# Attention heads taken two at a time: paired score matmuls, V as the stationary operand, outputs that arrive transposed

## The chip, the cores and the metric

The kernel runs on one core of one Trainium2 chip. The metric is device time in microseconds. A core has a matmul engine (PE, its weight loads listed apart as PEld), a vector engine (DVE), an activation engine (ACT), a general engine (POOL) and DMA queues (SP issues them); each executes its own instructions strictly in the order in which they were written to its queue, and waits on semaphores for the others.

## The reference

Two layers of an encoder on 256 tokens of width 1024. A layer is a half-step SwiGLU, a mixer, cross-attention to 256 memory tokens, a second half-step SwiGLU and a norm. Only the mixer and the cross-attention are touched here:

```
h = RMSNorm(x); z = h @ W_in                      # split among three groups of heads
A (mla): 8 heads, q and k of 96 columns, v of 64  # full softmax
B (swa): 4 heads of 64, 2 key heads, distance bias, one sink logit per head in the softmax sum
C (na):  4 heads of 64, neighbourhood bias per head
o = concat(RMSNorm(o_A, 512), RMSNorm(o_B, 256), RMSNorm(o_C, 256)) * g
x = x + o @ W_out
x = x + softmax(norm(q) norm(k)^T) v @ w_o        # 4 heads over 256 memory tokens
```

Every RMSNorm over a group divides a token's row by the root of its mean square over that group's columns.

## The kernel before

Everything stands in SBUF with 128 partitions; a 256 x 256 score matrix of a head is held as `[128, 2, 256]` (two blocks t of 128 queries, 256 keys). Weights come from memory as fp32 (`raw`) and are split on the chip into a high part (`whi`, ACT, line 140) and a low part (`wlo`, DVE, line 141); a product with weights is three matmuls (lines 167 to 169, and 528 to 530). The program is written in Python against a scheduler: each statement gives an instruction to an engine, and the scheduler fixes one order for each engine ahead of time. PSUM accumulators come from a pool of 8 (`acc`), 256-column working tiles from a pool of 8 (`b2`).

A layer l has a mixer (names `mx0...`, `mx1...`) and a memory attention (`me0...`, `me1...`); `kv0`, `kv1` is the memory's key and value projection, whose matmuls are interleaved with the mixer as hooks. In the mixer, `attend` goes through 16 heads in the order sw00, sw01, sw10, sw11 (swa), na00 to na11, ml00 to ml31 (mla). Head i's scores are issued at step i, the four 128 x 128 transposes of its probabilities at step i + d1 = i + 3, its products with V at step i + d2 = i + 5.

One head: two score matmuls into PSUM (`sc`, 64 rows of the array for swa, na and memory heads, 96 for mla). For swa and na the bias is added and the row maximum taken by one custom instruction for each t (line 447, into the separate tile `sb` and `mx`); for mla and memory by one reduction (line 441); `ng` is the negated maximum. ACT forms `p = exp(s - max)` in two calls (line 454) and, for swa, `es`, the sink's term (line 457). PE transposes p into `pt`; DVE copies it to `pT` in two copies (lines 467, 468). `values` then multiplies with pT as the stationary operand and V, 65 columns wide with a column of ones, as the moving one; so the softmax sum comes out as column 64. `finish`, once for two heads, takes the reciprocal `rc` and scales the output into `o` `[token, head column]` (line 418): nothing on DVE between a head's maximum and the next head's maximum depends on ACT.

`group_norm` squares o on ACT (line 844), forms the factor `om` on DVE (848) and `or` on POOL (line 173, a power), and scales o on DVE (852). `group_transposed` turns o over on PE (`ot`, line 864) and splits it into `oh` and `ol` (lines 176, 177). The table `AT` gives the steps at which these stand: norms at 9 and 12, transposes at 11 and 14; the norm of group A after the last head and its transposes inside the output projection. `project` multiplies with W_out (`mo`). The memory attention is the same with four heads a00, a01, a10, a11, outputs turned at line 930, split at 931 and 932, and `wo` as projection.

Of the kernel before, what the change touches and what calls it, by code (L numbers as in the profile page):

```python
# [9 lines left out]
F32 = mybir.dt.float32  # L10
# [8 lines left out]
P = 128  # L19
# [11 lines left out]
    d1=3, d2=5, look=3, norm1=9, turn1=11, norm2=12, turn2=14, turn0=20,  # L31
    keys=2, ksteps=3, knorm=3, kturn=13, v0=0, v1=13, e1=2, e2=4, wturn0=7, wturn1=6,
# [36 lines left out]
def encoder_kernel(ctx: ExitStack, tc: tile.TileContext, gxT, memT, wst, bparams, consts, nab, out):  # L69
# [36 lines left out]
    cmean = cp.tile([P, 3], F32, name="cmean")  # L106
    nc.vector.memset(cmean[:, 0:1], 1.0 / D)
    nc.vector.memset(cmean[:, 1:2], 1.0 / 256)
    nc.vector.memset(cmean[:, 2:3], 1.0 / 128)
    nhalf = cp.tile([P, 16], F32, name="nhalf")  # L110
# [284 lines left out]
    class Pair:  # L395


        def __init__(self, nm, o, cols):
            self.nm, self.o, self.cols = nm, o, cols
            self.pv, self.es = None, [None, None]  # L400

        def out(self, c):
            if self.pv is None:
                self.pv = acc(self.nm + "pv")[:, 0:260].rearrange("p (t c d) -> p t c d", t=2, c=2)
            return self.pv[:, :, c, :]

        def finish(self):
            pv = self.pv
            rc = small(4, self.nm + "rc").rearrange("p (t c) -> p t c", t=2)
            if self.es[0] is not None:  # L410
                dn = small(4, self.nm + "dn").rearrange("p (t c) -> p t c", t=2)
                for c in range(2):
                    nc.vector.tensor_tensor(dn[:, :, c], pv[:, :, c, 64], self.es[c], ALU.add)
                nc.vector.reciprocal(rc, dn)
            else:
                nc.vector.reciprocal(rc, pv[:, :, :, 64])
            for c in range(2):
                nc.vector.tensor_tensor(
                    self.o[:, :, self.cols[c], :], pv[:, :, c, 0:64], bc(rc[:, :, c], 64), ALU.mult
                )  # L420

    class Head:
        def __init__(self, pair, c, qT, kT, V, vh, prep=None, bias=None, sink=None):
            self.pair, self.c, self.qT, self.kT, self.V, self.vh = pair, c, qT, kT, V, vh
            self.prep = prep or (lambda: None)
            self.bias, self.sink = bias, sink
            self.nm = f"{pair.nm}{c}"
# [6 lines left out]
        def scores(self):  # L434
            nm = self.nm
            sc = acc(nm + "sc").rearrange("p (t k) -> p t k", t=2)
            for t in range(2):
                nc.tensor.matmul(sc[:, t, :], self.qT[:, t * P : (t + 1) * P], self.kT, start=True, stop=True)
            ng = small(2, nm + "ng")
            if self.bias is None:  # L440
                nc.vector.tensor_reduce(ng, sc, AX.X, ALU.max, negate=True)
                src = sc
            else:
                src = tp.tile([P, 2, T], F32, tag="b2", bufs=8, name=nm + "sb")
# [7 lines left out]
            self.p = tp.tile([P, 2, T], F32, tag="b2", bufs=8, name=nm + "p")  # L452
# [17 lines left out]
        def values(self):  # L470
            pv = self.pair.out(self.c)
            for t in range(2):
                for kt in range(2):
                    nc.tensor.matmul(
                        pv[:, t, :], self.pT[:, kt, t * P : (t + 1) * P], self.V[:, kt, self.vh, :],
                        start=kt == 0, stop=kt == 1,
                    )
            if self.c == 1:
                self.pair.finish()

    def attend(heads, hooks={}, d1=AT["d1"], d2=AT["d2"]):

        n = len(heads)
        heads[0].prep()
        for i in range(n + d2):
            if i + 1 < n:
                heads[i + 1].prep()
            if i < n:
                heads[i].scores()
                if i + 3 < n:  # L490
                    heads[i + 3].load()
            if 0 <= i - d1 < n:
                heads[i - d1].transposes()
            if 0 <= i - d2 < n:
                heads[i - d2].values()
# [48 lines left out]
    memV = cp.tile([P, 2, 4, 65], F32, name="memV")  # L544
    nc.gpsimd.memset(memV[:, :, :, 64:65], 1.0)
    memkT = cp.tile([P, 2, T], F32, name="memkT")

    class Memory:
# [62 lines left out]
        def values(self, n):  # L611
            if not self.at:
                self.ps = []
            self.steps("kvv", n, lambda t, ps: nc.scalar.activation(
                memV[:, t, :, 0:64], hd(ps[:, 0:256], 4), AF.Copy, scale=rmem[:, t : t + 1]
            ))

    def mixer(l, nx, mem):
# [32 lines left out]
        V = slot([P, 2, 14, 65], F32, nm + "V")  # L651
        nc.gpsimd.memset(V[:, :, :, 64:65], 1.0)
# [99 lines left out]
        for g in range(2):  # L752
            w = slice(512 * g, 512 * g + 512)
            for t in range(2):
# [8 lines left out]
                else:  # L763
                    nc.scalar.activation(V[:, t, 0:8, 0:64], hd(ps, 8), AF.Copy, scale=st)
# [69 lines left out]
        for h in heads[:3]:  # L834
            h.load()
# [295 lines left out]
```

## Time and profile before

| | us |
|---|---|
| median of 3 runs (lowest, highest) | 1047.52 (1047.47, 1062.58) |
| profiled execution | 1048.1 |
| its span, first to last instruction | 1046.3 |
| PE busy | 1024.0 (98%) |
| DVE busy | 718.0 (69%) |
| ACT busy | 556.7 (53%) |
| POOL busy | 114.2 (11%) |

The mean granted TensorE clock is 0.996 of full speed. In layer 0 the mixer's attention begins with its first score matmul at 236.29 us, the output projection runs from 282.79 to 307.03, the memory attention's projection begins at 331.10. In layer 1 the same points are at 752.91, 798.46, 822.70 and 846.65.

### The profile page before, as it was taken

Reading aid. Unit: us, or ns where it says so; the run is one execution under the profiler, and the core shown is the slowest. Engines: PE = TensorE matmul, PEld = TensorE weight load, DVE = VectorE, ACT = ScalarE, POOL = GpSimd, SP = SyncE. Lnnn points to the kernel's source line nnn. Section 1 sums busy time; section 2 is a strip of 40 time slices with the busy share of each in tenths; the row PEclk is TensorE's granted clock in tenths of the full one; section 3 lists DMA queues with packets and bytes.
Section 4 is the critical chain, followed back from the end, with each engine's and each line's share of the span. In section 5 each row is a group of like instructions: output and inputs, shape, how many; then the busy total and the mean of one; then the engine's idle time right before and its main releaser. Section 6 shows DMA issues by size and latency. Waiting matters only on the chain.

```text
span 1046.3 us, 20916 instructions
## 1 busy us (share of the span) xinstructions
PE 1024.0 (98%) x8480; PEld 1002.4 (96%) x8480; DVE 718.0 (69%) x1249; ACT 556.7 (53%) x928; POOL 114.2 (11%) x107
## 2 busy tenths in 40 slices
PE   8999999999999999999999999999999999999996
PEld 7999999998998999999999999999889999999996
DVE  7866667778786676666757666667886777766652
ACT  5755455566563565555545444546675546554541
POOL 4000000072031400000000000002600313000000
PEclk9999999999999999999999999999999999999998
DMA  8866666655042655555555555655531517666641
GB/s 277 276 208 192 198 199 206 186 173 182 22 136 67 234 189 199 188 199 192 192 184 187 188 186 184 206 186 167 181 131 32 172 38 241 204 189 196 194 130 41
DMA packets 54529, 181.79 MB, mean 174 GB/s; under 512 B 6048, under 2 KB 8992, under 8 KB 54432
## 3 DMA queue, kind: packets, MB, share of 16 engines
q1 hardware_dynamic: 54432, 180.45, 54.2%
q8 instruction: 66, 1.08, 0.4%
q14 instruction: 31, 0.25, 0.1%
HBM read 179.38 MB, written 1.05 MB: 172 GB/s over the span
## 4 chain that ended last, share of the span: by engine, by line
PE 72%; issue 17%; DVE 4%; POOL 2%; DMA 2%; ACT 2%; SPq 0%; POOLq 0%; DVEq 0%; ACTq 0%
PE f11i L169 4%; PE f11i L167 4%; PE f11i L168 4%; PE f01i L169 3%; PE f01i L167 3%; PE f01i L168 3%; PE f02i L168 3%; PE f02i L167 3%; PE f02i L169 3%; PE f11o L169 2%; PE f11o L167 2%; PE f11o L168 2%; PE f02o L169 2%; PE f01o L169 2%; PE f02o L168 2%
## 5 line engine op out<-in xcount | busy, mean ns | idle before, releaser
L141 DVE TENSOR_TENSOR wlo<-raw,whi 128x1024 fp32r<-128x1024 f32 (+4 forms) x337 | 407.5, 1214 | 208.9 <-ACT whi L140 207.7
L140 ACT CAST whi<-raw 128x1024 fp32r<-128x1024 f32 (+4 forms) x337 | 343.8, 1024 | 345.1 <-issue 86.0
L167 PE MATMUL f11i<-n10h,whi 128*128 128x256 f32 x320 | 90.1, 282 | 0.0
L168 PE MATMUL f11i<-n10l,whi 128*128 128x256 f32 x320 | 89.8, 281 | 0.0
L169 PE MATMUL f11i<-n10h,wlo 128*128 128x256 f32 x320 | 89.8, 281 | 0.0
L167 PE MATMUL f02i<-n20h,whi 128*128 128x256 f32 x320 | 88.5, 277 | 0.0
L167 PE MATMUL f01i<-n0h,whi 128*128 128x256 f32 x320 | 88.5, 277 | 0.0
L167 PE MATMUL f12i<-n21h,whi 128*128 128x256 f32 x320 | 88.5, 277 | 0.0
L169 PE MATMUL f01i<-n0h,wlo 128*128 128x256 f32 x320 | 88.4, 276 | 0.0
L168 PE MATMUL f02i<-n20l,whi 128*128 128x256 f32 x320 | 88.3, 276 | 0.0
L168 PE MATMUL f12i<-n21l,whi 128*128 128x256 f32 x320 | 88.3, 276 | 0.0
L169 PE MATMUL f02i<-n20h,wlo 128*128 128x256 f32 x320 | 88.3, 276 | 0.0
L168 PE MATMUL f01i<-n0l,whi 128*128 128x256 f32 x320 | 88.3, 276 | 0.0
L169 PE MATMUL f12i<-n21h,wlo 128*128 128x256 f32 x320 | 88.3, 276 | 0.0
L168 PEld LDWEIGHTS f11i<-n10l,whi 128*128 128x128 f32 x320 | 61.4, 192 | 0.0
L168 PEld LDWEIGHTS f12i<-n21l,whi 128*128 128x128 f32 x320 | 60.1, 188 | 0.0
L168 PEld LDWEIGHTS f02i<-n20l,whi 128*128 128x128 f32 x320 | 60.1, 188 | 0.0
L168 PEld LDWEIGHTS f01i<-n0l,whi 128*128 128x128 f32 x320 | 60.1, 188 | 0.0
L167 PEld LDWEIGHTS f01i<-n0h,whi 128*128 128x128 f32 x320 | 60.1, 188 | 0.0
L167 PEld LDWEIGHTS f11i<-n10h,whi 128*128 128x128 f32 x320 | 60.1, 188 | 0.0
L169 PEld LDWEIGHTS f01i<-n0h,wlo 128*128 128x128 f32 x320 | 60.1, 188 | 0.0
L167 PEld LDWEIGHTS f02i<-n20h,whi 128*128 128x128 f32 x320 | 60.1, 188 | 0.0
(1026 smaller groups left out, 2940.4 us busy)
## 6 DMA issues: line engine op xcount, KB each, us to landing
raw<-in_w SPq DMA_DIRECT2D x311, 512.0 KB, 4.2
raw<-in_w SPq DMA_DIRECT2D x12, 384.0 KB, 3.7
raw<-in_w SPq DMA_DIRECT2D x8, 416.0 KB, 3.3
kv0mt<-in_mem SPq DMA_DIRECT2D x8, 128.0 KB, 4.3
kv1mt<-in_mem SPq DMA_DIRECT2D x8, 128.0 KB, 3.7
gx<-in_gx SPq DMA_DIRECT2D x3, 256.0 KB, 7.2
out<-gx SPq DMA_DIRECT2D x3, 256.0 KB, 2.8
gx<-in_gx SPq DMA_DIRECT2D x1, 323.0 KB, 3.2
```

The costliest lines, as they stand in the source:

```text
L140: ins = nc.scalar.copy(hi[:, a:b], r[:, a:b])
L141: nc.vector.tensor_tensor(lo[:, a:b], r[:, a:b], hi[:, a:b].bitcast(F32), ALU.subtract)
L167: nc.tensor.matmul(ps, ah, bh, start=first, stop=False)
L168: nc.tensor.matmul(ps, ah, bl, start=False, stop=False)
L169: return nc.tensor.matmul(ps, al, bh, start=False, stop=last)
```

## The change

`Pair` now owns both heads of a pair. It issues the score matmuls of the two heads alternately (t = 0 of both, then t = 1 of both); for heads of 64 columns they lie in the two row halves of the array. `values` makes V (64 columns) stationary and pT (256 columns) moving, one head into PSUM partitions 0 to 63 and the other into 64 to 127; the result is `[feature, token]`, transposed from the outset. V and memV lose their column of ones. The softmax sum `dn` comes from the exponential's accumulator (`accum_out`); swa adds `es`; `rc` is taken for each head right after its exponentials, and p is multiplied by it in place, in two calls for each head, on POOL in the mixer and on DVE in the memory attention. The biased scores are written to p instead of `sb`. pT is copied in one instruction of 512 columns.

The outputs' own transposes (`ot`) are gone. The group norm now squares each pair's output on ACT (`osq`) beside a DVE copy to o, sums over features with matmuls of one column (`og`), forms `om` on DVE and `or` on POOL, spreads `or` over all partitions by two PE transposes (`ob`), and then multiplies on DVE and splits on ACT and DVE. Its hooks stand at steps 10 and 14, and inside the projection for group A. Rows of W_out and their gains are permuted on the host to the order in which the pairs put the heads.

```diff
+def mixed_order():
+    return np.concatenate([np.arange(512)] + [512 + 64 * h + np.arange(64) for h in (0, 2, 1, 3)] + [np.arange(768, 1024)])
...
-    d1=3, d2=5, look=3, norm1=9, turn1=11, norm2=12, turn2=14, turn0=20,
-    keys=2, ksteps=3, knorm=3, kturn=13, v0=0, v1=13, e1=2, e2=4, wturn0=7, wturn1=6,
+    d1=3, d2=5, look=3, norm1=10, norm2=14, norm0=4,
+    keys=2, ksteps=3, knorm=3, kturn=13, v0=0, v1=13, e1=2, e2=4,
...
+        def scores(self):
+            for h in self.heads:
+                h.sc = acc(h.nm + "sc").rearrange("p (t k) -> p t k", t=2)
+            for t in range(2):
+                for h in self.heads:
+                    nc.tensor.matmul(h.sc[:, t, :], h.qT[:, t * P : (t + 1) * P], h.kT, start=True, stop=True)
+            for h in self.heads:
+                h.weights()
+        def values(self):
+            pv = acc(self.nm + "pv")[:, 0:T]
+            for kt in range(2):
+                for c, h in enumerate(self.heads):
+                    nc.tensor.matmul(
+                        pv[64 * c : 64 * c + 64, :], h.V[:, kt, h.vh, :], h.pT[:, kt, :],
+                        start=kt == 0, stop=kt == 1,
+                    )
+            self.done(pv)
...
+            dn = small(2, nm + "dn")
             for t in range(2):
-                nc.scalar.activation(self.p[:, t, :], src[:, t, :], AF.Exp, bias=ng[:, t : t + 1])
+                nc.scalar.activation(
+                    self.p[:, t, :], src[:, t, :], AF.Exp, bias=ng[:, t : t + 1], accum_out=dn[:, t : t + 1]
+                )
             if self.sink is not None:
                 es = small(2, nm + "es")
                 nc.scalar.activation(es, ng, AF.Exp, bias=self.sink)
-                self.pair.es[self.c] = es
+                nc.vector.tensor_tensor(dn, dn, es, ALU.add)
+            rc = small(2, nm + "rc")
+            nc.vector.reciprocal(rc, dn)
+            for t in range(2):
+                self.eng.tensor_scalar(self.p[:, t, :], self.p[:, t, :], rc[:, t : t + 1], None, ALU.mult)
...
-            nc.vector.tensor_copy(self.pT[:, 0, :], ps[:, 0:T])
-            nc.vector.tensor_copy(self.pT[:, 1, :], ps[:, T : 2 * T])
+            nc.vector.tensor_copy(self.pT, ps.rearrange("p (k t) -> p k t", k=2))
...
+        def done(i):
+            def f(pv):
+                nc.vector.tensor_copy(o[:, i, :], pv)
+                osq[i] = b1(f"{nm}osq{i}")
+                nc.scalar.activation(osq[i], pv, AF.Square)
...
+            ps = acc(f"{nm}og{g}")
+            mean = cmean[:, 3:4] if g == 0 else cmean[:, 1:2]
+            for t in range(2):
+                for i in range(a, b):
+                    nc.tensor.matmul(
+                        ps[:, T + t : T + t + 1], osq[i][:, t * P : (t + 1) * P], mean, start=i == a, stop=i == b - 1
+                    )
+            om = small(2, f"{nm}om{g}")
+            nc.vector.tensor_scalar(om, ps[:, T : T + 2], EPS, None, ALU.add)
+            orr = small(2, f"{nm}or{g}")
+            rsqrt(orr, om, 2)
+            pb = acc(f"{nm}ob{g}")[:, 0:T]
+            for t in range(2):
+                nc.tensor.transpose(pb[:, t * P : (t + 1) * P], orr[:, t : t + 1].to_broadcast([P, P]), ident)
+            for i in range(a, b):
+                g_ = gn[:, l, G_GRP + i : G_GRP + i + 1]
+                nc.vector.scalar_tensor_tensor(o[:, i, :], o[:, i, :], g_, pb, ALU.mult, ALU.mult)
+                nc.scalar.copy(oT["h"][:, i, :], o[:, i, :])
+                nc.vector.tensor_tensor(oT["l"][:, i, :], o[:, i, :], oT["h"][:, i, :].bitcast(F32), ALU.subtract)
...
+        def done(b):
+            def f(pv):
+                nc.scalar.copy(oh[:, b, :], pv)
+                nc.vector.tensor_tensor(ol[:, b, :], pv, oh[:, b, :].bitcast(F32), ALU.subtract)
+            return f
```

Three places show what the change does to the order. On DVE, at the first two swa heads of layer 0 (the rows with ISA are the custom maximum and the read of its accumulator), before:

```order
L447 ISA mx0sw00sb,mx0sw00mx<-mx0sw00sc,mx0sw00bt,bp 128x256
L447 ISA mx0sw00mx 128x1
L141 TENSOR_TENSOR wlo_3716<-raw_3713,whi_3715 128x1024
L256 TENSOR_SCALAR kv0m<-kv0ps 128x2
L451 TENSOR_SCALAR mx0sw00ng<-mx0sw00mx 128x2
L589 TENSOR_SCALAR emem<-kv0m 128x2
L447 ISA mx0sw01sb,mx0sw01mx<-mx0sw01sc,mx0sw01bt,bp 128x256
```

and now, at the same place:

```order
L147 TENSOR_TENSOR wlo_3742<-raw_3739,whi_3741 128x1024
L456 TENSOR_SCALAR mx0sw00ng<-mx0sw00mx 128x2
L262 TENSOR_SCALAR kv0m<-kv0ps 128x2
L590 TENSOR_SCALAR emem<-kv0m 128x2
L465 TENSOR_TENSOR mx0sw00dn<-mx0sw00dn,mx0sw00es 128x2
L467 RECIPROCAL mx0sw00rc<-mx0sw00dn 128x2
L452 ISA mx0sw01p,mx0sw01mx<-mx0sw01sc,mx0sw01bt,bp 128x256
L452 ISA mx0sw01mx 128x1
```

Two instructions that read ACT's results for head sw00 (`dn` with `es`, then `rc`) now stand ahead of head sw01's maximum; at each of the 16 heads of both mixers its `rc` stands ahead of the next head's maximum in this way (`dn` at the swa heads only).

On POOL, late in layer 0's mixer, there were three `or` in a row before (`rmem` and `kv0f` belong to the memory's projection):

```order
L173 TENSOR_TENSOR rmem<-kv0m,nhalf 128x2
L173 TENSOR_TENSOR kv0f<-kv0m,nhalf 128x8
L173 TENSOR_TENSOR mx0or_3398<-mx0om_3396,nhalf 128x2
L173 TENSOR_TENSOR mx0or_3510<-mx0om_3508,nhalf 128x2
L173 TENSOR_TENSOR mx0or_3674<-mx0om_3672,nhalf 128x2
```

and now:

```order
L469 TENSOR_SCALAR mx0ml01p<-mx0ml01p,mx0ml01rc 128x256 x2
L469 TENSOR_SCALAR mx0ml10p<-mx0ml10p,mx0ml10rc 128x256 x2
L469 TENSOR_SCALAR mx0ml11p<-mx0ml11p,mx0ml11rc 128x256 x2
L179 TENSOR_TENSOR mx0or_3465<-mx0om_3463,nhalf 128x2
L469 TENSOR_SCALAR mx0ml20p<-mx0ml20p,mx0ml20rc 128x256 x2
L469 TENSOR_SCALAR mx0ml21p<-mx0ml21p,mx0ml21rc 128x256 x2
L469 TENSOR_SCALAR mx0ml30p<-mx0ml30p,mx0ml30rc 128x256 x2
L469 TENSOR_SCALAR mx0ml31p<-mx0ml31p,mx0ml31rc 128x256 x2
L179 TENSOR_TENSOR mx0or_3613<-mx0om_3611,nhalf 128x2
```

The first `or` now stands behind the scaling of head ml11, the second behind that of ml31, the last mla head.

On PE, at the end of the first eight heads' work in layer 0 (`qt` are the transposes that give heads ml20 and ml21 their q and k), now:

```order
L423 MATMUL mx0na0pv<-mx0na00pT,mx0V 64x256
L423 MATMUL mx0na0pv<-mx0na01pT,mx0V 64x256
L863 MATMUL mx0ob_3467<-ident,mx0or_3465 128x128 x2
L794 MATMUL mx0qt_3476<-ident,mx0qn 96x128
L795 MATMUL mx0qt_3476<-ident,mx0kn 96x128
```

Before, the piece of PE's order that prepares ml20 was this:

```order
L474 MATMUL mx0na1pv<-mx0V,mx0na10pT 128x65 x4
L864 MATMUL mx0ot_3463<-ident,mx0o 128x128
L794 MATMUL mx0qt_3472<-ident,mx0qn 96x128
L795 MATMUL mx0qt_3472<-ident,mx0kn 96x128
L794 MATMUL mx0qt_3472<-ident,mx0qn 96x128
```

In place of the transposes of o, the spreading of `or` (the first one of the POOL piece above) now stands ahead of the transposes for ml20 and ml21.

## Rows read from the trace of the kernel before

**Rows 1.** Busy time by stretch, layer 0's mixer: span, PE, PEld, DVE, ACT, POOL, clock, DMA

```profile
236.00:258.00 22.00, 21.47 (x150) 17.98 (x149) 18.92 (x68) 14.26 (x32) 3.15 (x3) 1.00 0.63 207
258.00:283.00 25.00, 25.00 (x203) 23.86 (x203) 20.91 (x63) 16.24 (x44) 3.04 (x3) 1.00 0.09 30
```

**Rows 2.** Waits of PE: what waited, for what, us in total, times, longest

```profile
PE mx0na00sc L438 <- DVE mx0sT L744: 0.5, 1, 0.5
PE me0wo L167 <- ACT me0oh L931: 0.5, 1, 0.5
```

**Rows 3.** Chain that ended last, 236 to 310 us: start, length, work

```profile
260.48 0.86 PE mx0ml01sc L438 x4
261.35 0.44 PE mx0na10pt L465 x4
261.78 0.84 PE mx0na0pv L474 x8
263.06 0.86 PE mx0ml10sc L438 x4
```

**Rows 4.** Timeline of PE, layer 0's mixer: start, length, line, operation, tiles

```profile
236.29 0.48 PE L438 MATMUL mx0sw00sc<-mx0sT 64*128 64x256 f32 x1
236.31 0.48 PE L438 MATMUL mx0sw01sc<-mx0sT 64*128 64x256 f32 x1
...
237.26 1.02 PE L438 MATMUL mx0sw10sc<-mx0sT 64*128 64x256 f32 x4
238.22 0.61 PE L251 MATMUL kv0ps<-cmean,kv0s 128*128 128x1 f32 x4
...
282.79 0.37 PE L167 MATMUL mx0mo<-mx0oh,whi 128*128 128x256 f32 x1
...
307.03 0.28 PE L169 MATMUL mx0mo<-mx0oh,wlo 128*128 128x256 f32 x1
```

**Rows 5.** Timeline of DVE, layer 0's mixer

```profile
239.87 0.47 DVE L447 CUSTOM_DVE_ANT_0 mx0sw00sb<-mx0sw00sc,mx0sw00bt,bp 128x256 f32<-128x256 f32 x1
...
240.68 1.22 DVE L141 TENSOR_TENSOR wlo<-raw,whi 128x1024 fp32r<-128x1024 f32 x1
...
241.89 0.15 DVE L451 TENSOR_SCALAR mx0sw00ng<-mx0sw00mx 128x2 f32<-128x2 f32 x1
...
242.08 0.48 DVE L447 CUSTOM_DVE_ANT_0 mx0sw01sb<-mx0sw01sc,mx0sw01bt,bp 128x256 f32<-128x256 f32 x1
...
256.48 0.17 DVE L451 TENSOR_SCALAR mx0na11ng<-mx0na11mx 128x2 f32<-128x2 f32 x1
```

**Rows 6.** Timeline of ACT, layer 0's mixer

```profile
242.08 0.91 ACT L454 ACTIVATE mx0sw00p<-mx0sw00sb,mx0sw00ng 128x256 f32<-128x256 f32 x2 [2.86 <-DVE mx0sw00ng L451]
242.89 0.28 ACT L457 ACTIVATE mx0sw00es<-mx0sw00ng,bp 128x2 f32<-128x2 f32 x1
...
264.85 0.20 ACT L844 ACTIVATION_READ_ACCUMULATOR mx0osq<-mx0o 128x1 f32 x1
```

**Rows 7.** Groups of DVE instructions, 236 to 283 us: busy us, mean ns, idle before

```profile
L767 DVE TENSOR_TENSOR mx0kn<-mx0uk,mx0fkf 128x512 f32<-128x512 f32 x2 | 1.3, 680 | 0.0
...
L744 DVE TENSOR_SCALAR mx0sT<-mx0st,gx 128x256 f32<-128x256 f32 x2 | 1.0, 476 | 0.0
...
L441 DVE TENSOR_REDUCE mx0ml30ng<-mx0ml30sc 128x2 f32<-128x512 f32 x1 | 0.7, 692 | 0.0
```

**Rows 8.** Groups of POOL instructions, 225 to 300 us

```profile
L173 POOL TENSOR_TENSOR mx0or<-mx0om,nhalf 128x2 f32<-128x2 f32 x3 | 2.1, 698 | 26.4 <-DVE mx0om L848 26.4
...
L717 POOL TENSOR_TENSOR mx0q<-mx0qn,mx0tab 128x256 f32<-128x256 f32 x1 | 1.7, 1725 | 0.0
...
L718 POOL TENSOR_TENSOR mx0q<-mx0qn,mx0tab 128x256 f32<-128x256 f32 x1 | 0.7, 746 | 0.0
```

**Rows 9.** Timeline of layer 0's memory attention: DVE's first maximum, PE's projection

```profile
322.43 0.69 DVE L441 TENSOR_REDUCE me0a00ng<-me0a00sc 128x2 f32<-128x512 f32 x1 [1.07 <-PE me0a01sc L438]
...
331.10 0.73 PE L167 MATMUL me0wo<-me0oh,whi 128*128 128x256 f32 x4 [0.52 <-ACT me0oh L931]
```

More of the change, by code (lines that the diff above doesn't have):

```diff
@@ L109, in encoder_kernel @@
     nc.vector.memset(cmean[:, 2:3], 1.0 / 128)
+    nc.vector.memset(cmean[:, 3:4], 1.0 / 512)
     nhalf = cp.tile([P, 16], F32, name="nhalf")
@@ L395, in encoder_kernel, with __init__ @@
     class Pair:
[L398 to L420, printed above, removed]
+        def __init__(self, nm, heads, done, eng=None):
+            self.nm, self.heads, self.done = nm, heads, done
+            for c, h in enumerate(heads):
+                h.nm, h.eng = f"{nm}{c}", eng or nc.gpsimd
@@ L432, in load, with weights @@
                 nc.sync.dma_start(self.bt, self.bias)
[L434 to L438, printed above, removed]
+        def weights(self):
+            nm, sc = self.nm, self.sc
             ng = small(2, nm + "ng")
+            self.p = tp.tile([P, 2, T], F32, tag="b2", bufs=8, name=nm + "p")
             if self.bias is None:
@@ L466, in transposes, with attend @@
             self.pT = tp.tile([P, 2, T], F32, tag="b2", bufs=8, name=self.nm + "pT")
-            nc.vector.tensor_copy(self.pT[:, 0, :], ps[:, 0:T])
-            nc.vector.tensor_copy(self.pT[:, 1, :], ps[:, T : 2 * T])
[L470 to L481, printed above, removed]
+            nc.vector.tensor_copy(self.pT, ps.rearrange("p (k t) -> p k t", k=2))
+    def attend(pairs, hooks={}, d1=AT["d1"], d2=AT["d2"]):
+        heads = [h for p in pairs for h in p.heads]
         n = len(heads)
-        heads[0].prep()
+        for h in heads[:2]:
+            h.prep()
         for i in range(n + d2):
[L486 to L491, printed above, removed]
+            if i % 2 == 1:
+                for h in heads[i + 1 : i + 3]:
+                    h.prep()
+            elif i < n:
+                pairs[i // 2].scores()
+                for h in heads[i + 4 : i + 6]:
+                    h.load()
             if 0 <= i - d1 < n:
                 heads[i - d1].transposes()
-            if 0 <= i - d2 < n:
-                heads[i - d2].values()
+            if 0 <= i - d2 < n and (i - d2) % 2 == 1:
+                pairs[(i - d2) // 2].values()
             for h in hooks.get(i, ()):
@@ L802, in mixer @@
         half = (slice(0, 64), slice(64, 128))
         swab = consts[:, 256 : 256 + 2048].rearrange("p (h t k) -> p h t k", h=4, t=2)
-        heads = []
+        pairs = []
         for pr in range(2):
-            pair = Pair(f"{nm}sw{pr}", o, [8 + pr, 10 + pr])
-            for c in range(2):
-                h = pr + 2 * c
-                heads.append(
-                    Head(
-                        pair, c, sT[half[c], pr, :], sT[half[c], 2, :], V, 8 + c,
-                        bias=swab[:, h], sink=bp[:, l, B_SINK + h : B_SINK + h + 1],
-                    )
-                )
+            pairs.append(Pair(f"{nm}sw{pr}", [
+                Head(
+                    sT[half[c], pr, :], sT[half[c], 2, :], V, 8 + c,
+                    bias=swab[:, pr + 2 * c], sink=bp[:, l, B_SINK + pr + 2 * c : B_SINK + pr + 2 * c + 1],
+                )
+                for c in range(2)
+            ], done(4 + pr)))
@@ L816, in mixer @@
         for pr in range(2):
-            pair = Pair(f"{nm}na{pr}", o, [12 + 2 * pr, 13 + 2 * pr])
             blocks = ((3, 5), (4, 6))[pr]
-            for c in range(2):
-                h = 2 * pr + c
-                heads.append(
-                    Head(
-                        pair, c, sT[half[c], 3 + pr, :], sT[half[c], 5 + pr, :], V, 10 + h,
-                        prep=(lambda b=blocks: prep_blocks(*b)) if c == 0 else None,
-                        bias=nab[l, :, h],
-                    )
-                )
+            pairs.append(Pair(f"{nm}na{pr}", [
+                Head(
+                    sT[half[c], 3 + pr, :], sT[half[c], 5 + pr, :], V, 10 + 2 * pr + c,
+                    prep=(lambda b=blocks: prep_blocks(*b)) if c == 0 else None, bias=nab[l, :, 2 * pr + c],
+                )
+                for c in range(2)
+            ], done(6 + pr)))
@@ L828, in mixer @@
+        latent = []
         for pr in range(4):
[L829 to L852 removed]
@@ L854, in group_transposed @@
-        def group_transposed(g):
+            hs = [Head(None, None, V, h, prep=lambda h=h: prep_latent(h)) for h in (2 * pr, 2 * pr + 1)]
+            latent += hs
+            pairs.append(Pair(f"{nm}ml{pr}", hs, done(pr)))
+        for pr in pairs[:2]:
+            for h in pr.heads:
+                h.load()
+        def group_norm(g):
             if not oT:
```

94 lines of the change are left out of this document (28 added, 66 removed).

## The prediction

> **What bounds the kernel now.** I read the table of stretches first, since the change touches only the mixers and the memory attention, some 160 us of the run. In the second half of layer 0's mixer attention PE is busy for all of 25.00 us and in the first half for 21.47 of 22; DVE has 18.92 and 20.91, ACT 14.26 and 16.24, POOL some 3 in each [rows 1]. PE's list of waits then shows that this is no chance: one wait in the mixer, 0.5 us for head na00, and one in the memory attention, 0.5 us ahead of its projection [rows 2]. The chain that ended last goes through PE alone here, with one mla head every 2.58 us (260.48 to 263.06): scores 0.86, transposes 0.44, values 0.84 and some q and k transposes [rows 3]. So PE is the bound, and DVE and ACT keep up with little room: DVE is 85% busy.
>
> What lets them keep up is in the timelines. DVE starts the maximum of sw00 at 239.87, negates it at 241.89, and at 242.08 it is on sw01, at the same moment at which ACT begins sw00's exponentials [rows 5, 6]. DVE and ACT overlap from head to head: na11's negation comes at 256.48, so eight heads take 16.6 us on DVE with weight splits of 1.22 us and copies among them.
>
> **PE's own work** falls. Two heads in the two row halves already run side by side in the trace: sw00 and sw01 start 0.02 us apart at 236.29 and are both through at 237.26, where sw10 alone takes 0.96 (237.26 to 238.22) [rows 4]. Before, only this pair went together; now sw1, na0 and na1 do as well, about 3 x 1.0 plus the changes of mode, 3.5 us a mixer. The mla heads, with 96 rows, gain nothing. Values cost 0.84 for a head [rows 3], 1.68 a pair. Now a head has two matmuls of 256 columns in fp32, each as long as one of the score matmuls, so 0.43 each; a pair takes 0.85 if the column halves run side by side as the row halves do, 1.7 if not. No row shows column halves; the ends are a saving of 0.83 a pair (6.6 us a mixer) and a loss of 0.3 with the mode changes (2.4). I take the row halves as the nearest row, less 0.3 a pair for the changes: 4.2 saved. Sixteen `ot` transposes go at 0.11 (0.44 for four [rows 3]): 1.75. Sixteen `og` matmuls of one column come at about 0.15 (four of this form take 0.61, the last one's tail included [rows 4]): 2.4; six `ob` 0.66. Net some 6.4 us less on PE in each mixer, and some 2.5 in each memory attention. If PE stayed the bound, that were the whole story.
>
> **What the change adds ahead of PE** is a wait of DVE on ACT in every head. `rc` of a head (and `dn` at swa heads) stands in DVE's order ahead of the next head's maximum; it needs the head's two exponentials with their accumulators; these need the head's negated maximum, which DVE has just made. DVE's next maximum is queued behind, and ACT, POOL and PE wait for that. The overlap of [rows 5, 6] is gone: heads go one after the other.
>
> A swa head then costs: two maximum passes 0.81 (239.87 to 240.68) and 0.2 from negation to exponential (241.89 to 242.08) [rows 5, 6]; exponentials 0.91, plus the accumulators' reads, seen at a square as 0.20 each [rows 6], of which I count one beside the next exponential, so 1.1; the sink's term 0.2 more (it starts at 242.89, 0.28 long); `dn` and `rc`, two small instructions of 0.15 to 0.17 as the negation's, with hand-over 0.3. Sum 2.6. A na head has neither sink nor `dn`: 2.2. Four of each are 19.2. DVE's order has more inside these cycles, between a maximum and its negation: two splits 2.44, two q/k copies 0.95, five of the 512-column pT copies, for which the 128x512 row of 0.68 stands [rows 5, 7]: 3.4; 6.8 together. What stands behind a negation is hidden under the exponentials. Eight heads: 26.0, so na11's `rc` ends at 239.87 + 26.0 = 265.9; its negation would be near 264.5, against 256.48: 8 us late.
>
> Four mla heads follow at 0.69 for the reduction [rows 7], 0.1, 1.1 and 0.15, so 2.0 each, and 0.7 of copies: ml11's `rc` at 274.6. Now the second wait. PE's next instruction after na0's values is `ob`, ahead of the q and k transposes of ml20 and ml21. `ob` needs the first `or`, on POOL behind the scaling of ml11. Scaling is 128x256 on POOL, one input and a factor per row; no row shows that form. The nearest is a 128x256 product of two tensors, 0.75 in one place and 1.73 in another of the same form [rows 8]; bounds are half of the quicker one (0.4, one input in place of two) and the slower. I take 0.75, since the two places follow each other on POOL with the same operands, and the slower one is the exception among [rows 8]. Then two scalings 1.5, `or` 0.70 [rows 8], hand-overs 0.3: `ob` at 277.1. The norm's `or` had POOL to itself before: it idled 26.4 us ahead of three of them [rows 8].
>
> From there ml20's q and k must be transposed (0.9), scaled on ACT, multiplied (0.9): its reduction starts at about 280.6. Four mla heads take 8.0 again and the second pair's q, k and scores some 1.5: ml31's `rc` at 290.1. The second `ob` (1.5 + 0.70 + 0.3) at 292.6. Behind it PE still has sixteen transposes of p 1.8, two pairs of values 1.7 and changes of mode: first `mo` at 296.8, against 282.79 [rows 4]: +14.0. In the output projection (24.2 us from 282.79 to 307.03) group A's norm adds eight `og` 1.2 and a wait for `om`, `or` and `ob` of 1.4, and eight `ot` leave, -0.9: +1.7. The late weight splits there add something under 1. So a mixer ends **+16.5 us**, twice +33. PE's saving of 6 us is not to be subtracted: it falls where PE waits.
>
> In the memory attention the same order holds with the scaling on DVE. From the first maximum at 322.43 [rows 9] four heads one after the other are 4 x 2.05 = 8.2 with the scalings hidden under the next exponentials, and `rc` of a11 at 330.7; then its scaling 0.85 (two of the 128x256 form, 0.48 less overlap [rows 7]), transposes 0.44, a copy 0.68, values and the split: the second half of the projection's input at about 334, the first, and with it `wo`, at 332.7 against 331.10 [rows 9]. The 18 matmuls of the first half cover part of the gap: +2.3 a layer (between 0 and 3.5), twice 4.6.
>
> Sum: 33 + 4.6 = 37.6 on 1048.1 us of the profiled execution, 0.6 above the median: **1085 us**. The feed-forward stages keep their orders and PE is full in them, so nothing is won back.
>
> **Rivals.** *The waits stay hidden and PE's work decides.* Price: -6.4 twice and -2.5 twice, -18, so 1030, not slower than before. It decides if a head's round from DVE to ACT and back, copies included, is shorter than PE's own work for a head, now some 2.1 us. Bare rounds of 2.0 to 2.6 speak against it, and copies lengthen them; for it speaks that the splits might fall where DVE now waits anyway. 8%.
>
> *The column halves don't run side by side.* Only values on the path count: three pairs after the last mla scores, and one or two that stand between mla heads, 0.85 each: +3 to +4 a mixer, +1 a memory attention: 1094. 17%.
>
> *POOL becomes the bound.* At 1.6 us, 32 scalings are 51 us from sw00's `rc` near 243.5, with `kv0f` and `or`. Then the twelve first heads are scaled by 284 in place of 276, the first `ob` comes 7 us later, and the last four heads' 12.8 us behind it put the second `ob` near 303 in place of 292.6: +10 a layer, 1105. For it speaks the 1.73 of one row of the same shape [rows 8]. 13%.
>
> A page of the Trainium skill makes this rival more precise: "SBUF — State Buffer", section "SBUF: two separate sides", says that a vector instruction with two SBUF inputs shuts a GpSimd instruction out of the shared port for its whole length. By it the 1.22 us splits would block scalings, but only for their own total in the stretch, some 7 us, so by that rule POOL would stay under the bound and the time near 1088. The trace agrees in so far as one shape has two durations; it doesn't show the split as the reason.
>
> For the second rival "TensorEngine Tiling (Array Packing)", section "Performance Considerations", promises up to twice the rate for column tiles of 64; no row here shows it, and by the rule the forecast's 0.85 a pair stands.
>
> **How the numbers follow.** Forecast 60%, PE alone 8%, column halves 17%, POOL 13%; 2% that the paired order does something else and ends near 1047. The likeliest gives 1085. The range reaches from 1062, where the first eight heads lose half of what I say and POOL is quick, to 1106. This kernel's runs tell no change from a change within about 2% (21 us): slower than 1068.5 takes nearly all of the forecast and its two dearer variants, 0.84; within 2% 0.13; faster 0.03.
>
> **What would show it.** In the changed kernel, `rc` of a head should be followed by the next head's maximum with DVE idle about 1 us in each head, released by ACT; PE should wait 4 to 7 us for the first `or`, 2 to 4 for the second; na11's exponentials should start near 264.5; first `mo` near 297 and 24 to 26 us of projection. I am wrong if DVE's idle time is spread elsewhere, if POOL's scalings are over 1 us, or if value matmuls of a pair start one after the other.

## The result and the profile after

The changed kernel takes 1108.36 us (median of 4 runs, 1102.87 to 1110.62) against 1048.47 (median of 4): a ratio of 1.0535, 95% interval 1.0451 to 1.0619. It is slower by some 60 us, where 37 were forecast. The profiled execution is 1102.87 us long, its span 1101.1 against 1046.3.

The first table is the one of stretches of the changed kernel, as in [rows 1] (span, PE, PEld, DVE, ACT, POOL, granted clock, DMA share, GB/s): the two stretches shown there, then layer 0's whole mixer from its first score matmul to its last `mo`, and the memory attention behind it.

```profile
236.00:258.00 22.00, 16.74 (x114) 13.25 (x112) 16.40 (x52) 12.85 (x34) 12.21 (x12) 0.89 0.61 183
258.00:283.00 25.00, 18.84 (x96) 14.32 (x97) 14.01 (x45) 13.74 (x46) 16.36 (x18) 0.77 0.16 51
...
236.83:333.30 96.47, 79.62 (x519) 66.28 (x519) 58.86 (x148) 48.24 (x131) 42.03 (x45) 0.86 0.28 87
333.30:366.50 33.20, 27.59 (x203) 23.32 (x202) 19.02 (x44) 12.08 (x32) 3.15 (x3) 0.90 0.20 66
```

The same two stages of the kernel before, for comparison:

```profile
236.29:307.14 70.85, 70.32 (x561) 1.00 0.35 112
...
307.14:337.20 30.06, 27.86 (x223) 25.85 (x222) 20.89 (x45) 11.75 (x25) 5.95 (x5) 1.00 0.27 89
```

No engine is full any more: PE, which was busy for 25.00 of 25 us, has 18.84, and DVE has fallen from 20.91 to 14.01. The mixer is 25.6 us longer (96.47 against 70.85), layer 1's 23.8 (93.70 against 69.90), the memory attentions 3.1 and 3.4; the feed-forward stages are as before. In the mixer PE idles 16.85 us in place of 0.53. That is not all: PE is also *busy* for 79.62 us in place of 70.32, with fewer instructions to do, and the clock column, 1.00 before, says 0.86.

PE's list of waits has in place of [rows 2] (what waited, for what, us in total, times, longest):

```profile
PE mx0ob L863 <- POOL mx0or L179: 9.6, 3, 5.2
PE mx1ob L863 <- POOL mx1or L179: 8.3, 3, 3.8
...
PE mx0sw00pt L476 <- POOL mx0sw00p L469: 2.7, 1, 2.7
...
PE me0a00pt L476 <- DVE me0a00p L469: 2.0, 1, 2.0
```

The first two lines are the spreading of `or`, behind POOL; the others are transposes of p that wait for its scaling. DVE's timeline shows where these come from (to be read beside [rows 5]):

```profile
244.05 0.17 DVE L467 RECIPROCAL mx0sw00rc<-mx0sw00dn 128x2 f32<-128x2 f32 x1
244.13 0.47 DVE L452 CUSTOM_DVE_ANT_0 mx0sw01p<-mx0sw01sc,mx0sw01bt,bp 128x256 f32<-128x256 f32 x1
...
246.86 0.16 DVE L465 TENSOR_TENSOR mx0sw01dn<-mx0sw01dn,mx0sw01es 128x2 f32<-128x2 f32 x1 [1.34 <-ACT mx0sw01es L464]
247.06 0.17 DVE L467 RECIPROCAL mx0sw01rc<-mx0sw01dn 128x2 f32<-128x2 f32 x1
247.14 0.47 DVE L452 CUSTOM_DVE_ANT_0 mx0sw10p<-mx0sw10sc,mx0sw10bt,bp 128x256 f32<-128x256 f32 x1
...
266.73 0.16 DVE L456 TENSOR_SCALAR mx0na11ng<-mx0na11mx 128x2 f32<-128x2 f32 x1
```

A swa head takes 3.01 us (244.13 to 247.14), in 1.34 of which DVE stands idle for ACT; before, the next head's maximum began the moment ACT began this head's exponentials. na11's negation comes at 266.73, not 256.48.

What the forecast didn't have is in PE's own rows behind a wait. The first lines are the clock by single microseconds around the first spreading (span, PE, clock, DMA share, GB/s), then PE's timeline from the first spreading of layer 0 to behind the third:

```profile
276.00:277.00 1.00, 0.00 (x0) 1.00 0.00 0
277.00:278.00 1.00, 0.00 (x0) 0.50 0.00 0
...
280.00:281.00 1.00, 1.00 (x6) 0.50 0.00 0
...
282.00:283.00 1.00, 1.00 (x6) 0.50 0.00 0
...
284.00:285.00 1.00, 1.00 (x6) 1.00 0.00 0
```

```profile
279.49 0.69 PE L863 MATMUL mx0ob<-ident,mx0or 128*128 128x128 f32 x2 [5.18 <-POOL mx0or L179]
279.97 0.42 PE L794 MATMUL mx0qt<-ident,mx0qn 128*96 128x128 f32 x1
280.18 0.42 PE L795 MATMUL mx0qt<-ident,mx0kn 128*96 128x128 f32 x1
...
282.53 1.67 PE L415 MATMUL mx0ml20sc<-mx0kT,mx0qT 96*128 96x256 f32 x4
284.04 1.03 PE L415 MATMUL mx0ml21sc<-mx0kT,mx0qT 96*128 96x256 f32 x4
...
296.75 0.43 PE L863 MATMUL mx0ob<-ident,mx0or 128*128 128x128 f32 x2 [3.36 <-POOL mx0or L179]
...
303.03 0.38 PE L173 MATMUL mx0mo<-mx0oh,whi 128*128 128x256 f32 x1
...
309.62 0.69 PE L863 MATMUL mx0ob<-ident,mx0or 128*128 128x128 f32 x2 [1.03 <-POOL mx0or L179]
...
310.75 0.41 PE L173 MATMUL mx0mo<-mx0oh,whi 128*128 128x256 f32 x1
310.96 0.41 PE L174 MATMUL mx0mo<-mx0ol,whi 128*128 128x256 f32 x1
...
314.57 0.28 PE L173 MATMUL mx0mo<-mx0oh,whi 128*128 128x256 f32 x1
314.69 0.28 PE L174 MATMUL mx0mo<-mx0ol,whi 128*128 128x256 f32 x1
```

PE waits 5.18 us; the granted clock falls from 1.00 to 0.50, that is from 2.4 to 1.2 GHz, and stays there for some four more microseconds after work has come back: transposes 0.21 us apart in place of 0.11, the scores of ml20 1.51 us ahead of ml21's in place of 0.86, and behind the third spreading `mo` matmuls 0.21 in place of 0.12. The Trainium skill describes this in "TensorE: Matmul & The Clock Gate", section "HAM oscillation — how this bites in real kernels": where PE waits again and again for DMA between bursts of matmuls, each burst begins at the low clock. The trace agrees for these waits on POOL, with 0.50 in these rows; but not every wait is followed by it: in experiment 12 PE idles 3.9 us of a mixer in many short waits, and the clock there is 1.00.

Two more of the forecast's open points can be read here. The column halves run side by side where both heads' pT are there, the second head 0.00 to 0.01 us behind the first; at sw0, whose second pT is copied later, they start one after the other. At ml2:

```profile
302.08 0.38 PE L423 MATMUL mx0ml2pv<-mx0ml20pT,mx0V 128*64 128x256 f32 x1
302.08 0.38 PE L423 MATMUL mx0ml2pv<-mx0ml21pT,mx0V 128*64 128x256 f32 x1
302.29 0.38 PE L423 MATMUL mx0ml2pv<-mx0ml20pT,mx0V 128*64 128x256 f32 x1
302.30 0.38 PE L423 MATMUL mx0ml2pv<-mx0ml21pT,mx0V 128*64 128x256 f32 x1
```

And a scaling on POOL takes 0.92 to 0.93 us in 14 of 16 heads (the row of one head; the longest mean is 1.24, at sw11), more than the 0.75 taken and far from 1.73:

```profile
L469 POOL TENSOR_SCALAR mx0na11p<-mx0na11p,mx0na11rc 128x256 f32<-128x256 f32 x2 | 1.8, 928 | 0.0
```

The long one is the second scaling of sw11: 1.54 us in either layer, and in both it begins while a weight split runs on DVE (in layer 0 it begins at 255.10, the split runs from 254.63 to 255.85). So does the 1.73 us product of [rows 8] in the trace of before (224.18; splits until 225.31), while no split begins or runs beside its quick neighbour of 0.75 (225.87). So the price of the POOL rival was that of a collision which here befell one scaling of 32 in a mixer.

### The profile page after: what moved, and what is told of

Its sections match the earlier page's. It is cut to its first block, busy times and chain, and to the rows that moved or that the text cites. A ratio compares the mean times of both kernels' runs of the same rounds, so it can differ in the third digit from the quotient of the medians.

```text
span 1101.1 us, 20814 instructions
## 1 busy us (share of the span) xinstructions
PE 1039.6 (94%) x8356; PEld 996.0 (90%) x8356; DVE 721.5 (66%) x1226; ACT 565.3 (51%) x1000; POOL 169.8 (15%) x168
## 3 DMA queue, kind: packets, MB, share of 16 engines
q8 instruction: 65, 1.06, 0.4%
## 4 chain that ended last, share of the span: by engine, by line
PE 65%; issue 17%; DVE 7%; ACT 4%; POOL 3%; DMA 3%; SPq 0%; POOLq 0%; DVEq 0%; ACTq 0%
PE f01i L174 3%; PE f11i L175 3%; PE f11i L174 3%; PE f11i L173 3%; PE f01i L173 3%; PE f01i L175 3%; PE f02i L175 3%; PE f02i L173 3%; PE f02i L174 3%; DVE wlo L147 2%; PE f02o L175 2%; PE f02o L174 2%; PE f02o L173 2%; PE f11o L175 2%; DMA raw<-in_w 2%
## 5 line engine op out<-in xcount | busy, mean ns | idle before, releaser
L173 PEld LDWEIGHTS f12i<-n21h,whi 128*128 128x128 f32 x320 | 60.1, 188 | 0.0
```

The lines of the kernel that those rows point to most:

```text
L173: nc.tensor.matmul(ps, ah, bh, start=first, stop=False)
```

## Experiments

Theory A: the rounds from DVE to ACT and back, one head after the other, are the main cost. Theory B: it is the place of the norm's spreading on PE. Theory C, from the rows above: PE's work at the low clock behind its waits is a cost of its own. Rivals: POOL is the bound; PE's work has grown.

**1. Reciprocals and scaling later.** In `weights` only the sum and `es` stay; the rest (`dn` plus `es`, reciprocal, scaling of p: `scaled`) stands behind the next pair's scores:

```diff
+            if i % 2 == 0 and 0 < i <= n:
+                for h in pairs[i // 2 - 1].heads:
+                    h.scaled()
             if 0 <= i - d1 < n:
                 heads[i - d1].transposes()
```

> The changed kernel, with each head's sum, reciprocal and scaling given out after the next pair's maxima, so that DVE no longer waits for ACT between two heads. If the serial rounds are the main cost, the first eight heads are some 8 us earlier in each mixer and the clock falls less often behind them: about 1108 - 2 x 13 = 1082 us. If the place of the norm's spreading (PE waiting for the first and second `or`) is the main cost, those waits stay and less than 8 us is gained: 1100 or more.

1107.07 us, ratio 1.0559 (1.0489 to 1.0630): nothing gained. DVE now waited for ACT only once at the swa heads (1.15 us, ahead of sw11's sum), but PE met p before it was scaled:

```profile
PE mx0sw00pt L481 <- POOL mx0sw00p L474: 5.7, 1, 5.7
...
PE mx0na10pt L481 <- POOL mx0na10p L474: 3.2, 1, 3.2
```

By its own numbers this speaks against A; but the sums had been moved one pair later while the transposes stayed three steps behind the scores, so the wait had only changed its place. That is what experiment 8 takes up.

**2. The spreading later.** The norm in two functions; the second (`ob` and what follows) at steps 12 and 16 and in the projection at 8:

```diff
+        def group_spread(g):
+            ...
+            (AT["turn1"], lambda: group_spread(1)), (AT["turn2"], lambda: group_spread(2)),
```

> The changed kernel, with the norm in two parts: sums and `or` at the old steps, the spreading and what follows two to four steps later, so that PE doesn't stand still for `or` ahead of the next heads' q and k. If the serial rounds are the main cost, the rounds then bound the last heads and 10 to 14 us are gained: about 1096. If the spreading's place is the main cost, the 9.6 and 8.3 us of its waits go, and the low clock behind them: about 1086.

1091.78 us, ratio 1.0379 (1.0331 to 1.0427), between the two. The waits for `or` fell from 9.6 and 8.3 to 3.7 and 3.9 us. So B is real, and worth 16.6 us; 40 are left.

**3. Filling in the wait, first try.** 11, 7 and 2 matmuls into the unused columns of the `og` bank ahead of `ob`.

```diff
+            for _ in range((2, 11, 7)[g]):
+                nc.tensor.matmul(ps[:, 0:T], ident, osq[a], start=True, stop=True)
```

> The changed kernel, with 11, 7 and 2 matmuls of 256 columns that nothing uses, put on PE right ahead of the three spreadings, to fill the waits there. If PE's idle time drops the granted clock and the work behind runs at half rate, the clock stays at 1.00 behind the first two, and some 2 us are saved at each: about 1101. If the low clock has another reason, or costs nothing since other engines bound the time there: 1108 or, with filling that overruns a wait, more.

1110.78 us, ratio 1.0557 (1.0503 to 1.0611). Inconclusive: the filling itself waited for DVE, which reads `om` from the same bank (`PE mx0og L862 <- DVE mx0om L858: 3.7` in PE's list of waits), so it didn't fill the first 2.5 us.

**4. The wait alone, in the kernel before.** Unused sums and reciprocals in `scores` of the kernel before:

```diff
-                nc.scalar.activation(self.p[:, t, :], src[:, t, :], AF.Exp, bias=ng[:, t : t + 1])
+                nc.scalar.activation(
+                    self.p[:, t, :], src[:, t, :], AF.Exp, bias=ng[:, t : t + 1], accum_out=dnx[:, t : t + 1]
+                )
             if self.sink is not None:
...
+                nc.vector.tensor_tensor(dnx, dnx, es, ALU.add)
+            nc.vector.reciprocal(small(2, nm + "rx"), dnx)
```

> The kernel before, with one thing added: the exponentials also accumulate their sums, and DVE adds the sink and takes a reciprocal for each head right away; nothing uses it. Order on DVE is then as in the changed kernel: a head's reciprocal ahead of the next head's maximum. If serial rounds are the main cost, this alone makes the kernel before 8 to 10 us slower in each mixer, with the memory attentions and the clock 20 to 28 us in all: about 1072. If they are hidden and other parts cost the time: under 6 us more, 1054.

1084.64 us, ratio 1.0298 (1.0234 to 1.0361): more than forecast, and over half of the whole loss from this alone. So A holds, with one reservation: the edit also gives DVE 2.9 us and ACT 3.4 us more work in the mixer (busy 57.80 for 54.93, 47.29 for 43.90), which was not tried apart; experiment 12 has the same sums and reciprocals at a later place and as much work on both, and its mixer takes 75.33 us where this one takes 81.76. How the time is lost is the surprise. Of the 10.9 us by which the mixer is longer, only 2.3 are idle time of PE; its busy time is 78.89 for 70.32. In the first mixer PE waits for only 1.1 and 1.8 us, and then (stretches of the same form as above):

```profile
248.00:252.00 4.00, 3.17 (x22) 1.00 0.34 116
252.00:256.00 4.00, 3.08 (x12) 0.67 0.76 264
256.00:260.00 4.00, 4.00 (x19) 0.50 0.43 144
...
264.00:268.00 4.00, 4.00 (x19) 0.50 0.18 56
268.00:272.00 4.00, 4.00 (x22) 0.69 0.00 0
```

it is busy without a gap at 1.2 GHz for some 17 us, and does 19 matmuls in 4 us where it does 33 from 272 to 276 us, at the full clock again.

**5. Filling that needs no other engine.** Matmuls of the identity with itself into the bank that the next real instruction writes anyway:

```diff
+            for _ in range({"sw00": 24, "sw01": 8, "sw11": 11, "na10": 8, "a00": 18, "a01": 9, "a10": 10, "a11": 12}.get(self.nm[3:], 0)):
+                nc.tensor.matmul(ps[:, 0:P], ident, ident, start=True, stop=True)
...
+            for _ in range((8, 46, 28)[g]):
+                nc.tensor.matmul(pb[:, T : T + P], ident, ident, start=True, stop=True)
```

> The changed kernel, with transposes of the identity that nothing uses put on PE ahead of the places where it waited: 24, 8, 11 and 8 ahead of the p transposes of heads sw00, sw01, sw11 and na10, 46, 28 and 8 ahead of the three spreadings, 18, 9, 10 and 12 in the memory attention, each about as much PE time at full clock as the wait there; they need no other engine, unlike the filling tried first. If part of the loss is PE's work at the lower clock behind its waits, the granted clock stays at 1.00 and 15 to 20 us of 1108 come back: about 1090. If DVE, ACT and POOL bound the time there anyway, or the clock falls for another reason: 1108 or more.

1136.35 us, ratio 1.0821 (1.0767 to 1.0874). The size was wrong: one filling is two passes, 0.225 us and not 0.11 (`276.88 10.54 PE L865 MATMUL mx0ob<-ident 128*128 128x128 f32 x92` in PE's timeline), so it outlasted the waits by 10 to 15 us a mixer. But the clock was 1.00 in every stretch of the mixer, and of PE's 97.23 us there the 133 fillings are 29.9, which leaves 67.3 for its own work.

**6. Only the score matmuls in pairs**, in the kernel before:

```diff
+            for t in range(2):
+                for h in hs:
+                    nc.tensor.matmul(h.sc[:, t, :], h.qT[:, t * P : (t + 1) * P], h.kT, start=True, stop=True)
```

> The kernel before, with only the score matmuls of each two heads issued alternately, as in the change; values, sums, norms and outputs as before. If row halves give what sw00 and sw01 already show, PE saves some 3.5 us a mixer and 1 in a memory attention and no new wait comes: 1048 - 9 = 1039 to 1042. If the earlier second head only moves waits: 1048.

1050.44 us, ratio 0.9995 (0.9968 to 1.0022): the same. PE's busy time in layer 0's mixer falls from 70.32 to 68.67 us, but the mixer takes 71.30 in place of 70.85:

```profile
235.80:307.10 71.30, 68.67 (x561) 1.00 0.33 112
```

The saving is half of what was reckoned (1.65 for 3.5) and turned into waits of PE for DVE and ACT, which had little room in [rows 1].

**7. Scaling on DVE in place of POOL** (`eng or nc.vector`).

> The changed kernel, with the scaling of p in the mixer on DVE in place of POOL. The norm's `or` then has POOL to itself and a scaling takes 0.4 us in place of 0.93, so the path from a head's reciprocal to its transposes is 1 us shorter; DVE gets 13 us more a mixer, partly beside exponentials. If POOL's place in the chain costs (scaling and `or` behind it): about 1092. If the serial rounds of DVE and ACT alone decide: 1108 or more.

1105.08 us, ratio 1.0510 (1.0456 to 1.0565): no different from the changed kernel. A scaling there is 0.35 us, POOL is down to 12.42 us of the 95.2 us mixer, and the waits for `or` are still 6.8 us in each. DVE got 7.8 us more in exchange, so this alone doesn't clear POOL; but in the changed kernel itself POOL is busy for 42.03 of 96.47 us and mostly stands idle until the next `rc` comes (7.0 us ahead of ml20's scaling, 2.0 ahead of ml30's). So POOL was not the bound of the changed kernel.

**8. Late reciprocals, late spreading, and two more steps** between a head's scores and its transposes and values (d1=5, d2=7, spreading at 14 and 18).

> The changed kernel with late sums and reciprocals as in the first experiment, the spreading late as in the second, and the transposes and values of a head two steps later (5 and 7 steps behind its scores in place of 3 and 5), so that the longer path from scores to scaled p has other heads' work beside it. If that path was too long for three steps, PE's waits nearly go, the clock stays up, and PE's smaller work shows: 1035 to 1050. If buffers or DVE, ACT and POOL's work bound the mixer: over 1080.

1083.60 us, ratio 1.0335 (1.0262 to 1.0408). The mixer is 83.0 us long, PE idles 10.2 of it. Now POOL is in the way; its rows ahead of the second `or`:

```profile
280.88 2.04 POOL L474 TENSOR_SCALAR mx0ml21p<-mx0ml21p,mx0ml21rc 128x256 f32<-128x256 f32 x2
282.90 1.82 POOL L474 TENSOR_SCALAR mx0ml30p<-mx0ml30p,mx0ml30rc 128x256 f32<-128x256 f32 x2
284.70 1.82 POOL L474 TENSOR_SCALAR mx0ml31p<-mx0ml31p,mx0ml31rc 128x256 f32<-128x256 f32 x2
286.49 0.72 POOL L179 TENSOR_TENSOR mx0or<-mx0om,nhalf 128x2 f32<-128x2 f32 x1
```

One after the other without a gap, and PE waits 3.3 us for that `or`.

**9. Experiment 4 with its waits filled**: 5 matmuls of the identity with itself ahead of na00's scores, 8 ahead of sw00's values, 2 and 3 in the memory attention, at 0.225 us.

> The kernel before with the unused sums and reciprocals of the fourth experiment (1084.6 us), and with transposes of the identity that nothing uses on PE where it waited there: 5 ahead of head na00's scores and 8 ahead of sw00's values in each mixer, 2 and 3 in a memory attention, 0.225 us each, so about PE's 3 us of waits and 1 us. If those waits cost mainly by the lower clock behind them (1.2 GHz for some 15 us in each mixer), the clock stays at 1.00 and most of the loss goes: about 1056 to 1062. If the serial rounds themselves hold PE up, filling changes nothing: 1084.

1067.30 us, ratio 1.0169 (1.0131 to 1.0208), so 17 us back by giving PE *more* to do. The same stretches as in experiment 4:

```profile
248.00:252.00 4.00, 4.00 (x31) 1.00 0.36 92
252.00:256.00 4.00, 4.00 (x33) 1.00 0.84 254
256.00:260.00 4.00, 3.40 (x25) 1.00 0.59 182
```

C holds here: about half of the 33 us comes back (by the ratios 1.3 of 3.0%) once the clock stays up.

**10. Experiment 8 with the scaling shared**: t = 0 on POOL, t = 1 on DVE; the norm's steps 11 and 15, the spreading at 14 and 20, in the projection 6 and 16.

```diff
-                self.eng.tensor_scalar(self.p[:, t, :], self.p[:, t, :], rc[:, t : t + 1], None, ALU.mult)
+                (self.eng, nc.vector)[t].tensor_scalar(self.p[:, t, :], self.p[:, t, :], rc[:, t : t + 1], None, ALU.mult)
```

> The deeper kernel of the eighth experiment (1083.6 us), with the scaling of p shared: first query block on POOL, second on DVE; and with the norm's sums one step earlier and its spreading later (two steps for the second group, in the projection at units 6 and 16 in place of 4 and 8). There POOL was busy for 29 us of 26 to 29 with scalings of 0.92 us, and PE waited 3.3 us for the second `or` behind them. If POOL was the bound, half of that goes, PE's waits fall under 3 us a mixer and the clock stays up: 1050 to 1060. If DVE now is the bound: 1080 or more.

1068.04 us, ratio 1.0151 (1.0111 to 1.0190): better than experiment 8 by some 16 us, less than hoped. No wait for `or` is left in the list's first places; PE waits 2.6 us for na00's keys and 2.5 for the last pair's p.

**11. The changed kernel with half of experiment 5's filling** (12, 4, 6, 4; 23, 14, 4; 9, 4, 5, 6).

> The changed kernel with half of the filling of the fifth experiment, where one filling took 0.225 us (two passes) and not 0.11, so that it outlasted the waits: now 12, 4, 6 and 4 ahead of the p transposes, 23, 14 and 4 ahead of the spreadings, 9, 4, 5 and 6 in the memory attention. If part of the loss is PE's work at the lower clock behind waits, the clock stays near 1.00 and 12 to 20 us of 1108 come back: about 1093. If the other engines bound the time all through: 1108 or more.

1093.25 us, ratio 1.0415 (1.0376 to 1.0454): 15 us faster than the changed kernel (13 by the ratios), with nothing changed but useless work on PE.

```profile
235.70:323.50 87.80, 84.17 (x653) 72.58 (x653) 53.83 (x141) 44.90 (x128) 39.38 (x44) 1.00 0.27 85
```

Of the 84.17 us, 67 fillings at 0.225 are 15.1, so PE's real work at the full clock is 69.1 us, where the changed kernel needed 79.62.

**12. Experiment 10, mended**: na00's q and k prepared one pair earlier, the last pair's reciprocals one step earlier, and filling where PE may still wait (4, 7; 9 and 4 in the memory attention).

> The kernel of the tenth experiment (1068 us) with what its trace still shows mended: na00's q and k prepared one pair earlier (PE waited 2.6 us for them), the last pair's reciprocals one step earlier (2.5 us ahead of ml30's transposes), and unused transposes of the identity where PE may still wait: 4 ahead of na00's scores, 7 ahead of ml30's transposes, 9 and 4 in the memory attention. In that kernel PE idles 6.5 us a mixer and loses some 4 more at the lower clock; if these two are all that is left of the loss, some 9 a layer go: 1048 to 1052, level with the kernel before, or faster. If DVE, ACT and POOL hold it up elsewhere: 1060 or more.

1060.78 us, ratio 1.0093 (1.0058 to 1.0127): the best of the paired kernels, and still some 1% slower than the kernel before.

```profile
235.70:311.03 75.33, 71.46 (x542) 1.00 0.31 105
```

The mixer is 4.5 us longer than before: 3.9 of idle time against 0.5, 2.5 of filling (11 at 0.225), and 69.0 us of work against 70.32.

## Why the prediction came out as it did

The direction was right and so was the cause as far as it went; the size was not: 1108 against 1085, with the median 2 us above the upper end of the range and the profiled execution 3 below it.

**The serial rounds: right.** Experiment 4 gives them alone 33 us, about half of it by the clock (experiment 9). A swa head took 3.0 us where 2.6 was reckoned without what stands inside the cycle, and na11's negation was at 266.73 where "near 264.5" stood (0.5 of the difference is a later start of the mixer). DVE's idle time per head, said to be about 1 us, was 1.1 to 1.4 at three of the swa heads; at sw11 a weight split fills it.

**The wait for `or`: right.** Forecast 4 to 7 us for the first and 2 to 4 for the second; measured 5.18 and 3.36. Experiment 2 showed its place is worth 16.6 us, though a third of these waits stayed. POOL's scaling was mis-sized, 0.92 for 0.75, some 0.35 a head.

**The idle time: fewer waits than the working implies.** A mixer 16.5 us longer with 6.4 us less work on PE would have PE idle for some 22.9 us more. Its idle time rose by 16.3 us in layer 0 and 18.0 in layer 1. That these lie near 16.5 is chance; the mixer grew by 25.6 and 23.8.

**The step that failed** is that PE's work was priced at the full clock throughout, as in the sentence "PE's saving of 6 us is not to be subtracted: it falls where PE waits": the sum has no term for work that gets dearer behind a wait. It got dearer: PE is busy for 79.62 us in layer 0 with what takes 69.0 to 69.1 at the full clock by experiments 11 and 12 and 67.3 by experiment 5, so 10.6 to 12.3 us were lost at 1.2 GHz. The changed kernel's own trace says the same: in its half-microsecond stretches PE is busy for 22.7 us at a clock of 0.50, and half of that is 11.3. In layer 1 (75.73 us busy) the two ways give 6.7 to 8.4, and 8.0. So of the +25.6 us of the mixer +16.3 are idle time and +9.3 busy time, the low clock less what was saved. With +23.8 in layer 1 and +3.1 and +3.4 in the memory attentions, where 2.3 was reckoned, the span's +54.8 is covered within 1.1 us. The trace of before could not give a price for this: its clock was 1.00 in every stretch around the change.

The same can be followed along the forecast's own path in layer 0, with 0.5 us taken off for the later start. The mixer was behind its forecast by 1.7 us at na11's negation, by 1.9 at the first `ob`, by 3.1 at ml20's reduction (284.24 where 280.6 stood), by 3.6 at the second `ob`, by 5.7 at the first `mo` (303.03 where 296.8 stood), and by 9.1 at its end, the projection having taken 30.3 us in place of 24 to 26. Three of these steps, 1.2, 2.1 and 3.4 us, lie behind the first and second spreading and in the projection around the third. There PE's rows are at 1.2 GHz for 3 to 5 us each time, which costs about half of that: the q and k transposes and the scores of ml20 took 1.71 and 1.51 us where 0.9 and 0.9 stood. The first 1.7 us are rounds that were longer than reckoned.

**PE's saving: mis-sized.** 6.4 us a mixer were reckoned from parts; 1.3 were there by experiments 11 and 12, 3.1 by experiment 5. Values fell as reckoned (a pair 1.06 with the change of mode, 255.97 to 257.03 in experiment 12's timeline, for 1.68), but a one-column `og` matmul is two passes, 0.22 in place of 0.15 (3.5 us for sixteen; the four rows read at 0.61 were two matmuls), and pairing the scores gave 1.65 of 3.5. The three don't add up to the whole difference; what remains, 1 to 3 us, I haven't traced.

**The rivals.** *PE alone decides* is refuted by the waits, and even experiment 12, with the waits nearly gone, leaves PE 1 to 3 us a mixer to win. *Column halves one after the other* is refuted by their rows. *POOL the bound* is refuted for the changed kernel by its idle time there and by experiment 7, though its price of 1105 lies nearer to the result than the forecast's: the right number by the wrong mechanism. Its rows speak for it in experiment 8, where the rounds are gone; experiment 10 takes half of the scaling off POOL and moves the norm's steps with it, so the two weren't tried apart.

**Open:** that experiment 1 gained nothing because its transposes met p unscaled is read from where PE's waits stood, not tried apart from the rounds (experiment 8 changes both); of the 6.4 us by which experiment 9's mixer (77.20 us in layer 0) is still longer than before, 2.9 are its 13 fillings and 1.8 idle time; 1.6 us more of busy time stay unexplained.

## What to carry to other kernels

Where one engine is full and two others keep up by running a head ahead of each other, a small instruction that reads back the second engine's result ahead of the first one's next head can cost the whole overlap, however short it is; place such a step behind the next head's first instruction, and give the chain behind it as many more steps as it has grown, or the wait only moves. Where the bound engine is TensorE, price a wait twice: once as idle time, and once as the work behind it at half the clock, if the granted clock shows that it fell. A few useless matmuls that fit the wait show in one run how much of a loss is of the second kind; if they outlast it, as in experiment 5, they cost more than they give.

## What the runs showed of the hardware

Three microseconds of waits in a mixer were followed by some 17 us at 1.2 GHz in which PE's rows show no gap (experiment 4), and with 13 small fillings in the waits the clock stayed at 1.00 (experiment 9). Two heads in the column halves start 0.00 to 0.05 us apart and take 1.06 us with the change of mode; in the form before, with 65 columns moving and one head after the other, they took 1.68. A 128x256 multiplication by a factor per row is 0.92 us on POOL and 0.35 on DVE, and on POOL slower than a product of two tensors of that shape (0.75); on POOL it took 1.54 us where it began while a weight split ran on DVE, in both layers.
